# Seven-product FFN units whose products add onto copies that ScalarE writes into PSUM, with PSUM banks in two groups and four changes of order

## The chip, the cores and the metric

The kernel runs on one core of one Trainium2 chip. A core has TensorE (PE: matrix products from SBUF into PSUM; PEld are its weight loads), VectorE (DVE), ScalarE (ACT), GpSimd (POOL) and SyncE (SP), which only issues DMA transfers. Each engine takes its instructions in the order in which they were written for it; engines wait for each other by semaphores. PSUM has 8 banks of 512 fp32 columns in 128 partitions. The metric is the device time of one execution in microseconds. The kernel before takes 1118.08 us, the median of 3 runs (1117.55 to 1118.87).

## The reference

One layer of a decoder trunk over 16 meta tokens and 512 real ones, width 1024, in fp32: an FFN, a token mixer with two attention branches, and a second FFN.

```python
def swiglu(h, w_in, w_out):                      # D_FF = 2816
    gu = h @ w_in                                # (tokens, 1024) @ (1024, 5632)
    gate, up = jnp.split(gu, 2, axis=-1)
    return (jax.nn.silu(gate) * up) @ w_out

def reference(x, meta_tokens, ...):
    ...
    h = h + 0.5 * swiglu(rms_norm(h, ffn1_norm[l]), ffn1_w_in[l], ffn1_w_out[l])
    h = h + token_mixer(rms_norm(h, mix_norm[l]), ...)   # fox and sliding-window attention, gates, w_out
    h = h + 0.5 * swiglu(rms_norm(h, ffn2_norm[l]), ffn2_w_in[l], ffn2_w_out[l])
    return h[:, BLOCK:]                          # the 512 real tokens
```

The gate and up products of both FFNs are the part that the change touches most.

## The kernel before, in words

**Precision.** Every fp32 operand is split into a high part, rounded to the float32r type, and a low part, the rest. `hi` (line 114) is a ScalarE copy with rounding (its instructions show line 117, or 118 with a scale), `lo` (line 120) a VectorE subtraction (line 124, or 126). `prod` (line 246) is three matmuls: high x high (L250), high x low (L251), low x high (L253).

**Weights as pieces.** `pieces` is the list of all weight pieces in the order of use. `load_to` issues their DMA transfers into tiles `raw` (three buffers), `split_to` makes `wh` and `wl` of them (three buffers each), and `piece()` takes the next one, splitting up to three pieces ahead and loading up to five ahead. `tc.issue_after(i)` puts what is written inside it behind instruction `i` on that engine's queue. Apart from that, a planner orders each engine's instructions by the order of the program and by a model of when each can start.

**FFN units.** An FFN makes 22 units of 128 gate and 128 up features for all tokens (528 in the first FFN, 512 in the second). The first 4 (3 in the second FFN) are *plain*: for each half of the tokens, gate and up products over the 1024 input features. The others are *seven-product units* (`Units.unit`, line 448). The tokens are cut into two halves of 264 (256) and the features into two halves of 512, so the input is A11, A12, A21, A22 (token half, feature half), and the weights of the unit are B11, B21 (gate) and B12, B22 (up). Strassen's scheme in Winograd's form makes the 2 x 2 block product in seven products instead of eight, with S1 to S4 for sums of A blocks, which are made once (`Halves.sums`, line 368), and with sums of B blocks, made per unit. Each product is 4 feature blocks x 3 matmuls = 12 matmuls of 264 (256) columns.

The unit's products run in the order A11, A12, S3, S1, S2, A22, S4. P1 = A11 B11 goes to bank b, is copied into SBUF (`p1`, L456) and stays in b, where the S2 product is added to it and gives U2. VectorE then puts the results together: `g` = A12's product + p1, d - p7, minus U2, c + U2, times the SiLU, S4's bank minus U2, times the SiLU: seven operations (`tt`, L450), and the low part of the result. ScalarE does three copies (p1, p7, u2), two SiLUs, and the high part.

**The sums of B blocks.** `sums` (line 177): piece A is the gate block as it is (B11, B21). For B SyncE loads half of the gate and half of the up block side by side into a tile `tb`, and a GpSimd DMA that accumulates adds the 512 KB of the up block onto it (L185). C is made by two VectorE additions (L189, L190), and D is B22.

**PSUM.** One pool of 8 banks serves the whole kernel; `psum()` (line 111) takes the next free one.

**Order around the units.** In `early` (line 647) the plain units are interleaved with the making of the second token half and of S1 to S4, by `weave`, which spreads one list of steps evenly over another. The units come in three groups (8, 8 and 6 units, `KG`), each followed by the product with `w_out` (first FFN lines 705 to 735: 8 output blocks, two banks each; second FFN lines 1410 to 1429: token tiles of 128 x 512 columns, whose results are added to the residual by L1425 and, in the last group, written to `out` in halves of 256 by SyncE and ScalarE queues). In the attention part `fills` (line 1260) lists projection steps that are woven between the steps of the attention: `qb0` and `qb1` are the query projections of the sliding-window branch; the last step of each transposes its normed result. `spread`, `tok_rms`, `features` and `to_features` (lines 304 to 623) make the normed and transposed input at the entry.

Of the kernel before, what the change touches and what calls it, by code (L numbers as in the profile page):

```python
# [73 lines left out]
def kernel(  # L74
# [28 lines left out]
    pp = ctx.enter_context(tc.tile_pool(name="ps", bufs=8, space=PSUM))  # L103
# [7 lines left out]
    def psum():  # L111
        return pp.tile([P, 512], F32, tag="ps", name=nm("ps"))
# [20 lines left out]

    def ffn_pieces(wi, wo, token_major):
        nc_ = NC[token_major]
        for gi, (j0, n) in enumerate(KG):
            for u in range(2 * j0, 2 * (j0 + n)):
                if u < nc_:
                    pieces.extend([("w", [(wi[u], 8, 128)]), ("w", [(wi[NU + u], 8, 128)])])
                else:  # L140
                    pieces.extend([("A", wi[u]), ("B", wi[NU + u]), ("C",), ("D",)])
# [28 lines left out]
    def load(*parts):  # L170
        raw = wp.tile([P, PW], F32, tag="raw", name=nm("raw"))
        for c0, ap in parts:
            i = SP.dma_start(raw[:, c0 : c0 + 128 * ap.shape[1]], ap)
            shared["load"] = getattr(i, "ins", i)
        return raw

    def sums(g, u, gate, up):

        tb_, tc_ = (
            shared["tp"].tile([P, shared["w"]], F32, tag=t, name=nm(t), bufs=2)[:, :1024].rearrange("p (a c) -> p a c", c=512)  # L180
            for t in ("tb", "tc")
        )
        SP.dma_start(tb_[:, 0], gate[:, :4])
        SP.dma_start(tb_[:, 1], up[:, :4])
        G.dma_start(tb_.rearrange("p a c -> p (a c)"), up, accum_op=ALU.add)  # L185

        def rest():
            b21, b22 = g[:, 512:1024], u[:, 512:1024]
            V.tensor_tensor(out=tc_[:, 0], in0=tb_[:, 0], in1=b22, op=ALU.add)  # L189
            V.tensor_tensor(out=tc_[:, 1], in0=tc_[:, 0], in1=b21, op=ALU.add)  # L190
            return tc_.rearrange("p a c -> p (a c)"), 8, 128

        return tb_, rest

    def load_to(n):
        while state["load"] < min(n, len(pieces)):
# [14 lines left out]
            elif kind == "A":  # L211
                shared["g"], shared["gate"] = load((0, what[0])), what[0]
                raws[c] = (shared["g"][:, :1024], 8, 128)
            elif kind == "B":
                g = shared["g"]
                u = load((512, what[0][:, 4:]))
                tb_, rest = sums(g, u, shared["gate"], what[0])
                raws[c] = (tb_.rearrange("p a c -> p (a c)"), 8, 128)
                raws[c + 1] = rest
                raws[c + 2] = (u[:, 512:1024], 4, 128)  # L220

    def split_to(n):
        while state["split"] < min(n, len(pieces)):
# [8 lines left out]
            wh = wp.tile([P, PW], F32R, tag="wh", name=nm("wh"))  # L232
            wl = wp.tile([P, PW], F32R, tag="wl", name=nm("wl"))
# [100 lines left out]
    class Halves:  # L334
# [27 lines left out]
        def diff(self, tag, a, b, op=ALU.subtract):  # L362
            t = shared["tp"].tile([P, shared["w"]], F32, tag=tag, name=nm(tag), bufs=2)
# [4 lines left out]
        def sums(self):  # L368
# [3 lines left out]
            def s3():  # L372

                s["done"] = getattr(self.done, "ins", self.done)
                with tc.issue_after(s["done"]):
                    d = self.diff("tb", self.of(0, 0), self.of(1, 0))
# [7 lines left out]
            def s2():  # L384
                s[2] = self.diff("tb", s[1], self.of(0, 0))
# [7 lines left out]
    class Units:  # L393


        def __init__(self, pool, X):
            self.pool, self.X, self.th = pool, X, X.th
# [17 lines left out]
        def plain(self, dst, mixed):  # L415
# [5 lines left out]
            def part(t, gu, half):  # L421
# [4 lines left out]
                if half == 0:  # L426
                    box["ps", gu] = psum()
# [20 lines left out]
        def unit(self, aH, aL):  # L448
            th = self.th
            tt = lambda o, a, b, op: V.tensor_tensor(out=o, in0=a, in1=b, op=op)  # L450
            u2 = self.new("u2", 1)
            w = piece()
            b, a = psum(), psum()
            self.product(b, "A11", w, 0)
            p1 = self.new("p1", 2)
            A.copy(p1, b[:, :th])  # L456
            self.product(a, "A12", w, 1)
            g = self.new("g", 2)
            tt(g, a[:, :th], p1, ALU.add)
            s1 = self.new("s1", 2)  # L460
# [1034 lines left out]
```

## Time and profile before

| | |
|---|---|
| median of 3 runs | 1118.08 us (1117.55 to 1118.87) |
| the profiled execution | 1117.38 us |
| its span, first to last instruction | 1115.6 us |
| instructions in the span | 20330, of them 8143 matmuls |
| granted TensorE clock | full in all 40 slices |
| GpSimd-issued (accumulating) DMA, queue q0 | 19.48 MB |

The profile is of one execution. A matmul's row shows from when it starts to when its last column is out, so neighbouring rows overlap, and the distance of two starts is the cadence. A row of a group reads: line, engine, operation, output<-inputs by tile name, shape, count | time in all, mean ns of one | idle time of the engine ahead of them, and what ended it. A row of a timeline reads: start us, length us, engine, line, operation, names, shape, count, and in brackets the idle time ahead and what ended it. A row of waits reads: who <- for whom: us in all, times, the longest.

### The profile page before, as it was taken

To read this page: it belongs to the slowest core of one execution; us is meant where nothing else is said; L and a number is where in the kernel's file an instruction comes from. 1 tells how busy PE (TensorE), PEld (TensorE's weight loads), DVE (VectorE), ACT (ScalarE), POOL (GpSimd) and SP (SyncE) were. 2 spreads that over 40 slices of the span, in tenths; PEclk is the share of its full clock that TensorE was granted. 3 is DMA by queue.
4 is the path that set the end of the run, shared out by engine and by line. 5 is a ranking of instruction groups with operands and counts; after the bars stand their busy time and mean duration, and the time that the engine had idled before them with its cause. 6 is when DMAs were issued, how large, how long until landed. Compare 5 with 4: busy or idle time off the path is not lost.

```text
span 1115.6 us, 20330 instructions
## 1 busy us (share of the span) xinstructions
PE 1106.4 (99%) x8143; PEld 1041.2 (93%) x8143; DVE 757.0 (68%) x1416; ACT 527.6 (47%) x941; POOL 84.0 (8%) x119
## 2 busy tenths in 40 slices
PE   8999999999999999999999999999999999999998
PEld 7999999999999999999887888899999899988996
DVE  6757348863687567788877655678685378835872
ACT  6446125541455455456555633355464155623550
POOL 2000000000000321221200000000000000000000
PEclk9999999999999999999999999999999999999999
DMA  7548337872464522212211224455566257733742
GB/s 232 149 128 229 100 95 189 206 221 66 123 162 133 164 77 95 80 58 69 87 57 58 76 76 151 151 177 147 132 173 177 66 159 176 202 125 87 190 131 76
DMA packets 57279, 146.45 MB, mean 131 GB/s; under 512 B 8224, under 2 KB 13344, under 8 KB 57184
## 3 DMA queue, kind: packets, MB, share of 16 engines
q1 hardware_dynamic: 43376, 114.95, 32.1%
q0 software_dynamic: 5456, 19.48, 10.4%
q10 hardware_dynamic: 8352, 10.72, 3.0%
q8 instruction: 64, 1.05, 0.4%
q14 instruction: 31, 0.25, 0.1%
HBM read 140.89 MB, written 6.32 MB: 132 GB/s over the span
## 4 chain that ended last, share of the span: by engine, by line
PE 94%; ACT 2%; DVE 2%; issue 0%; POOL 0%; DVEq 0%; ACTq 0%; POOLq 0%
PE ps L250 29%; PE ps L251 29%; PE ps L253 29%; PE ps L1173 1%; PE ps L1051 1%; PE ps L1006 1%; ACT t L966 1%; PE ps L1066 1%; ACT wh L117 1%; PE ps L288 1%; PE ps L1184 1%; PE ps L1065 0%; PE ps L1185 0%; PE ps L924 0%; DVE wl L124 0%
## 5 line engine op out<-in xcount | busy, mean ns | idle before, releaser
L250 PE MATMUL ps<-x,wh 128*128 128x264 f32 (+2 forms) x1388 | 408.7, 295 | 0.4 <-ACT wh L117 0.3
L251 PE MATMUL ps<-x,wh 128*128 128x264 f32 (+2 forms) x1388 | 407.3, 294 | 0.5 <-DVE x L126 0.4
L253 PE MATMUL ps<-x,wl 128*128 128x264 f32 (+2 forms) x1388 | 406.4, 293 | 0.0
L117 ACT CAST wh<-raw 128x1024 fp32r<-128x1024 f32 (+2 forms) x193 | 183.5, 952 | 246.4 <-PE ps L251 108.4
L124 DVE TENSOR_TENSOR wl<-raw,wh 128x1024 fp32r<-128x1024 f32 (+2 forms) x193 | 212.9, 1104 | 91.2 <-ACT wh L117 89.9
L250 PEld LDWEIGHTS ps<-x,wh 128*128 128x128 f32 x1388 | 261.7, 189 | 7.9 <-ACT x L117 0.8
L251 PEld LDWEIGHTS ps<-x,wh 128*128 128x128 f32 x1388 | 261.3, 188 | 6.0 <-DVE x L126 0.9
L253 PEld LDWEIGHTS ps<-x,wl 128*128 128x128 f32 x1388 | 261.5, 188 | 5.5
L251 PE MATMUL ps<-aL,wh 128*128 128x264 f32 x352 | 93.3, 285 | 0.0
L250 PE MATMUL ps<-aH,wh 128*128 128x264 f32 x352 | 93.1, 285 | 0.0
L250 PE MATMUL ps<-wh,x 128*128 128x256 f32 (+1 forms) x288 | 83.6, 290 | 0.0
L251 PE MATMUL ps<-wl,x 128*128 128x256 f32 (+1 forms) x288 | 81.7, 284 | 0.0
L253 PE MATMUL ps<-wh,x 128*128 128x256 f32 (+1 forms) x288 | 81.3, 282 | 0.0
L253 PE MATMUL ps<-aH,wl 128*128 128x264 f32 x352 | 71.5, 284 | 0.0
L250 PE MATMUL ps<-wh,aH 128*128 128x512 f32 x176 | 69.7, 396 | 0.0
L251 PE MATMUL ps<-wl,aH 128*128 128x512 f32 x176 | 69.2, 393 | 0.0
L253 PE MATMUL ps<-wh,aL 128*128 128x512 f32 x176 | 69.0, 392 | 0.0
L124 DVE TENSOR_TENSOR wl<-tb,wh 128x1024 fp32r<-128x1024 f32 x37 | 45.4, 1226 | 32.9 <-ACT wh L117 31.9
L117 ACT CAST wh<-tb 128x1024 fp32r<-128x1024 f32 x37 | 38.9, 1050 | 59.0 <-PE ps L251 45.7
L251 PEld LDWEIGHTS ps<-aL,wh 128*128 128x128 f32 x352 | 66.2, 188 | 0.1
L250 PEld LDWEIGHTS ps<-aH,wh 128*128 128x128 f32 x352 | 66.2, 188 | 0.0
L721 DVE SCALAR_TENSOR_TENSOR hT<-ps,hT 128x264 f32<-128x264 f32 x48 | 18.6, 427 | 62.1 <-PE ps L253 62.1
(243 smaller groups left out, 1864.6 us busy)
## 6 DMA issues: line engine op xcount, KB each, us to landing
raw<-in_w1i_dram SPq DMA_DIRECT2D x26, 512.0 KB, 3.8
raw<-in_w2i_dram SPq DMA_DIRECT2D x25, 512.0 KB, 3.4
raw<-in_w2o_dram SPq DMA_DIRECT2D x22, 512.0 KB, 4.1
tb<-in_w2i_dram SPq DMA_DIRECT2D x38, 256.0 KB, 3.2
tb<-in_w2i_dram POOLq DMA_DIRECT2D x19, 512.0 KB, 6.9
tb<-in_w1i_dram SPq DMA_DIRECT2D x36, 256.0 KB, 3.5
tb<-in_w1i_dram POOLq DMA_DIRECT2D x18, 512.0 KB, 6.9
raw<-in_wm_dram SPq DMA_DIRECT2D x18, 512.0 KB, 4.2
```

The lines of the kernel that those rows point to most:

```text
L117: return A.copy(o, i)
L124: return V.tensor_tensor(out=o, in0=i, in1=h, op=ALU.subtract)
L250: PE.matmul(ps, sH, mH, start=first, stop=False, **more)
L251: PE.matmul(ps, sH, mL, start=False, stop=False, **more)
L253: shared["mm"] = PE.matmul(ps, sL, mH, start=False, stop=last, **more)
L288: PE.matmul(idle[:, :P], ident, ident, start=True, stop=True)
L721: V.scalar_tensor_tensor(out=hv, in0=p[:, :w], scalar=0.5, in1=hv, op0=ALU.mult, op1=ALU.add)
L966: A.activation(t, t, AF.Exp, bias=nmx, scale=-1.0, accum_out=l[:, j : j + 1])
L1006: PE.matmul(ps[:, :w], q[qx][hb, hp, P * i : P * i + P], k[kx][hb, hp, c0 : c0 + w], start=qx + kx == 0, stop=qx == 1 and not last,)
L1051: PE.transpose(ps[:, c : c + P], ts_[hh][(c // P) % 2][:, c0 : c0 + P], ident)
L1066: PE.matmul(pv[:, a:256], st, pL[:, c0 + a : c0 + 256], start=False, stop=j == nt - 1)
L1173: PE.transpose(ps[:n, P * hh : P * hh + P], ts_[hh][:, c0 : c0 + n], ident)
```

## The change

**The unit** becomes `seven` (products) and a `use` function (what is done with each result). The order of the products is A11, S3, [S4 of the unit before], S2, A22, A12, S1, and S4 is kept pending and done inside the next unit (`flush`). In the last unit of each group the order is S1, A12, S4 at the end. ScalarE copies P1 from bank b into bank a, and the A12 product is added onto the copy. ScalarE writes -U2 into bank d, and the S1 product and later the S4 product are added onto that. VectorE is left with four operations (c + U2, d - p7, two products with a SiLU) and the low part. ScalarE reads one SiLU right from PSUM.

**Banks.** `new_banks(True)` makes two groups of four banks, tags `ps` and `pt`; a and d, onto which ScalarE writes, are from `pt`. The attention part has one pool of eight (`new_banks(False)`), the second FFN two groups again.

**Pieces.** A is now (B11, B12-B22 sum), B the sums made by VectorE, C the loaded block with one sum, D as before. SyncE issues four transfers and GpSimd two accumulating ones of 256 KB a unit. D has its own split buffers (`whD`, `wlD`), the VectorE sums one buffer (`tc`).

**Four changes of order.** The last unit of a group (order of products, and the splits of the next two pieces written behind it); the fills of the attention; one empty step ahead of the S sums of the second FFN; the last token tile of the kernel as two halves of 256 columns in two banks.

```diff
-    pp = ctx.enter_context(tc.tile_pool(name="ps", bufs=8, space=PSUM))
+    def new_banks(split):
+        stP.close()
+        banks["pool"] = stP.enter_context(tc.tile_pool(name=nm("banks"), bufs=4 if split else 8, space=PSUM))
+        banks["split"] = split
+    def psum(whole=False):
+        tag = "pt" if whole and banks["split"] else "ps"
+        return banks["pool"].tile([P, 512], F32, tag=tag, name=nm(tag))
...
+    def load_first(b1, b2, n):
+        raw = wp.tile([P, PW], F32, tag="raw", name=nm("raw"))
+        land(raw, b1[:, :n])
+        land(raw[:, 128 * n :], b2[:, :n])
+        add(raw[:, 128 * n :], b2[:, n:])
+        return raw[:, : 256 * n], 2 * n, 128
+    def load_others(b1, b2, n):
+        w = 128 * n
+        fpool = shared["tp"]
+        c = fpool.tile([P, PW], F32, tag="rawC", name=nm("rawC"), bufs=2)
+        d = fpool.tile([P, 512], F32, tag="rawD", name=nm("rawD"), bufs=2)
+        land(c, b1)
+        add(c, b2[:, :n])
+        land(d, b2[:, n:])
+        def sums():
+            t = fpool.tile([P, PW], F32, tag="tc", name=nm("tc"), bufs=1)
+            V.tensor_tensor(out=t[:, :w], in0=c[:, :w], in1=d[:, :w], op=ALU.add)
+            V.tensor_tensor(out=t[:, w : 2 * w], in0=t[:, :w], in1=c[:, w : 2 * w], op=ALU.add)
+            return t[:, : 2 * w], 2 * n, 128
+        return sums, (c[:, : 2 * w], 2 * n, 128), (d[:, :w], n, 128)
...
+            if pieces[c][0] == "D":
+                wh, wl = (shared["tp"].tile([P, 512], F32R, tag=t, name=nm(t), bufs=1) for t in ("whD", "wlD"))
...
-    def piece():
+    def piece(ahead=None):
...
-        split_to(c + state["ahead"])
+        split_to(c + (ahead or state["ahead"]))
...
-        def unit(self, aH, aL):
...
+        def seven(self, use, last=False):
+            th = self.th
+            w = piece()
+            b, a = psum(), psum(True)
+            self.product(b, "A11", w, 0)
+            A.copy(a[:, :th], b[:, :th])
+            c = psum()
+            self.product(c, "S3", w, 1)
+            use("P7", c[:, :th])
+            self.flush()
+            w = piece()
+            self.product(b, "S2", w, 0, True)
+            d = psum(True)
+            A.activation(d[:, :th], b[:, :th], AF.Identity, scale=-1.0)
+            use("U2", b[:, :th])
+            self.product(c, "A22", w, 1, True)
+            use("C21 - U2", c[:, :th])
+            w = piece()
+            def p2():
+                self.product(a, "A12", w, 1, True)
+                use("C11", a[:, :th])
+            def p5():
+                self.product(d, "S1", w, 0, True)
+                use("C22 + P7", d[:, :th])
+            run([p5, p2] if last else [p2, p5])
+            wd = piece(1 if last else None)
+            def p3():
+                self.product(d, "S4", wd, 0, True)
+                use("C12", d[:, :th])
+            self.pending = p3
+            if last:
+                self.flush()
+        def unit(self, dst, last=False):
+            th, box = self.th, {}
+            tt = lambda o, a, b, op: V.tensor_tensor(out=o, in0=a, in1=b, op=op)
+            def use(what, ps):
+                if what == "P7":
+                    box["p7"] = self.new("p7", 1)
+                    A.copy(box["p7"], ps)
+                elif what == "U2":
+                    box["u2"] = ps
+                elif what == "C21 - U2":
+                    u2 = self.new("u2", 1)
+                    A.copy(u2, box["u2"])
+                    g = self.new("g", 1)
+                    tt(g, ps, u2, ALU.add)
+                    box["s2"] = self.new("s2", 2)
+                    A.activation(box["s2"], g, AF.Silu)
+                elif what == "C11":
+                    box["s1"] = self.new("s1", 2)
+                    A.activation(box["s1"], ps, AF.Silu)
+                elif what == "C22 + P7":
+                    o = box["o"] = self.new("u", 2, 2)
+                    tt(o[:, th:], ps, box["p7"], ALU.subtract)
+                    tt(o[:, th:], o[:, th:], box["s2"], ALU.mult)
+                else:
+                    o = box["o"]
+                    tt(o[:, :th], ps, box["s1"], ALU.mult)
+                    aH, aL = dst
+                    hi(aH, o)
+                    lo(aL, o, aH)
+            self.seven(use, last)
+            if last:
+                split_to(state["use"] + 2)
...
-        pss = [psum() for _ in ks]
+        pss = [psum(k % 2 == 0 or hf == 0 and k == 7) for k in ks]
...
+    new_banks(False)
     kp = ctx.enter_context(tc.tile_pool(name="keep", bufs=1))
...
-        kv[LAG:-1] + qb0[:LAG] + kv[-1:] + qb0[LAG:-1] + qb1[:LAG] + qb0[-1:],
-        qb1[LAG:-1] + gates[:LAG] + qb1[-1:] + gates[LAG : 2 * KD],
+        kv[LAG:-1] + qb0[:LAG] + kv[-1:] + qb0[LAG:-1] + qb1[:2] + qb0[-1:] + qb1[2:4],
+        qb1[4:-1] + gates[:LAG] + qb1[-1:] + gates[LAG : 2 * KD],
...
+    new_banks(True)
     def token_major(i):
...
-    early(X2, ff2, [lambda u=u: act2(u) for u in range(NC[1])], second, X2.sums(), [])
+    early(X2, ff2, [lambda u=u: act2(u) for u in range(NC[1])], second, [nothing] + X2.sums(), [])
...
-            ff2.unit(*act2(u))
+            ff2.unit(act2(u), u == 2 * (j0 + n) - 1)
...
+            ends = [gi == len(KG) - 1 and mq == 1 and i == NB - 1 for i in range(NB)]
+            pss = [[psum(f == 1)[:, :256] for f in range(2)] if e else [psum(i % 2 == 1)] for i, e in enumerate(ends)]
```

More of the change, by code (lines that the diff above doesn't have):

```diff
@@ L132, with seven_pieces @@
     pieces = []
+    def seven_pieces(b1, b2, n):
+        pieces.extend([("A", b1, b2, n), ("B", b1, b2, n), ("C",), ("D",)])
     def ffn_pieces(wi, wo, token_major):
@@ L140, in ffn_pieces @@
                 else:
[L141 removed]
+                    seven_pieces(wi[u], wi[NU + u], 4)
             if token_major:
@@ L168, with land, add @@
     shared = {}
-    def load(*parts):
-        raw = wp.tile([P, PW], F32, tag="raw", name=nm("raw"))
[L172 to L193, printed above, removed]
+    def land(tile_, ap):
+        i = SP.dma_start(tile_[:, : 128 * ap.shape[1]], ap)
+        shared["load"] = getattr(i, "ins", i)
+    def add(tile_, ap):
+        G.dma_start(tile_[:, : 128 * ap.shape[1]], ap, accum_op=ALU.add)
+    def load_first(b1, b2, n):
+        raw = wp.tile([P, PW], F32, tag="raw", name=nm("raw"))
+        land(raw, b1[:, :n])
[16 more added lines that the diff above has]
+        return sums, (c[:, : 2 * w], 2 * n, 128), (d[:, :w], n, 128)
     def load_to(n):
@@ L211, in load_to @@
             elif kind == "A":
-                shared["g"], shared["gate"] = load((0, what[0])), what[0]
-                raws[c] = (shared["g"][:, :1024], 8, 128)
+                raws[c] = load_first(*what)
             elif kind == "B":
[L215 to L220, printed above, removed]
+                raws[c], raws[c + 1], raws[c + 2] = load_others(*what)
     def split_to(n):
@@ L446, in plain, with flush @@
             ]
-        def unit(self, aH, aL):
+        def flush(self):
+            f, self.pending = self.pending, nothing
+            f()
+        def seven(self, use, last=False):
             th = self.th
-            tt = lambda o, a, b, op: V.tensor_tensor(out=o, in0=a, in1=b, op=op)
-            u2 = self.new("u2", 1)
             w = piece()
-            b, a = psum(), psum()
+            b, a = psum(), psum(True)
             self.product(b, "A11", w, 0)
[L455 to L460, printed above, removed]
-            A.activation(s1, g, AF.Silu)
-            w = piece()
-            c, d = psum(), psum()
-            self.product(c, "S3", w, 1)
-            p7 = self.new("p7", 1)
-            A.copy(p7, c[:, :th])
-            self.product(d, "S1", w, 0)
-            o = self.new("u", 2, 2)
-            tt(o[:, th:], d[:, :th], p7, ALU.subtract)
+            A.copy(a[:, :th], b[:, :th])
+            c = psum()
+            self.product(c, "S3", w, 1)
+            use("P7", c[:, :th])
+            self.flush()
@@ L489 @@
+    shared["tp"] = fp
     xn = hT
@@ L695 @@
             later = [residual(u - 3)] if u < 8 else []
-            ff1.unit(*act1(u))
+            ff1.unit(act1(u), u == 2 * (j0 + n) - 1)
             run(later)
@@ L706 @@
             wH, wL = piece()
-            pss = [psum() for _ in hs]
+            pss = [psum(f == 1) for f in range(2)]
             for k in range(nk):
@@ L1424 @@
                     hv = h2[:, i, 512 * mq + c : 512 * mq + c + w]
-                    V.scalar_tensor_tensor(
-                        out=hv, in0=pss[i][:, c : c + w], scalar=0.5, in1=hv, op0=ALU.mult, op1=ALU.add
-                    )
+                    ps = pss[i][1] if ends[i] and c else pss[i][0][:, c : c + w]
+                    V.scalar_tensor_tensor(out=hv, in0=ps, scalar=0.5, in1=hv, op0=ALU.mult, op1=ALU.add)
                     if gi == len(KG) - 1:
```

53 lines of the change are left out of this document (23 added, 30 removed).

## The prediction, made before the changed kernel was run

> **What bounds the kernel now.** I read the first page of the profile first (spans, busy shares, the chain that ended last), then busy time by stretch, then what TensorE waited for, and last the groups of instructions inside a stretch of the seven-product units.
>
> ```profile
> span 1115.6 us, 20330 instructions
> PE 1106.4 (99%) x8143; PEld 1041.2 (93%) x8143; DVE 757.0 (68%) x1416; ACT 527.6 (47%) x941; POOL 84.0 (8%) x119
> ```
>
> ```profile
> PE 94%; ACT 2%; DVE 2%; issue 0%; POOL 0%; DVEq 0%; ACTq 0%; POOLq 0%
> ```
>
> TensorE is busy 1106.4 of 1115.6 us and the chain that ended last lies on it for 94%. So 9.2 us in all are not TensorE time. The stretches tell where they lie, and how full the other engines are in one unit.
>
> ```profile
> 26.50:376.00 349.50, 349.50 (x2872) 349.27 (x2872) 231.86 (x359) 158.93 (x249) 18.77 (x28) 1.00 0.55 151
> 376.00:560.00 184.00, 182.63 (x1531) 173.93 (x1530) 140.00 (x404) 100.10 (x240) 41.59 (x57) 1.00 0.27 83
> 560.00:777.00 217.00, 216.53 (x1271) 186.49 (x1270) 148.34 (x278) 102.51 (x182) 2.34 (x3) 1.00 0.35 112
> 777.00:1111.50 334.50, 334.50 (x2323) 311.14 (x2321) 218.39 (x334) 147.51 (x232) 15.44 (x18) 1.00 0.52 141
> 1111.50:1115.60 4.10, 0.25 (x2) 0.00 (x0) 0.76 (x2) 0.00 (x0) 0.00 (x0) 1.00 0.38 128
> 295.40:305.60 10.20, 10.20 (x86) 10.20 (x85) 8.71 (x15) 6.28 (x12) 0.86 (x1) 1.00 0.47 135
> ```
>
> The last row is from a second answer of the same view. Columns are length, then busy time of TensorE, its weight loads, VectorE, ScalarE and GpSimd, the granted clock, the DMA share. All 37 seven-product units lie in 26.5 to 376 and in 777 to 1111.5 (both FFNs behind their first steps), and there TensorE is busy 349.50 of 349.50 and 334.50 of 334.50 us at a clock of 1.00. The last row is one such unit: TensorE full, VectorE 8.71 of 10.20 us, ScalarE 6.28. VectorE is the fuller of the two, but TensorE never waits for it here. Idle time is left in the attention stretch (1.37 us), in 560 to 777 (0.47), after the last matmul (3.85), and in the first 26.5 us (the remaining 3.5).
>
> ```profile
> PE ps L288 <- POOL ident masks.py:199: 2.2, 1, 2.2
> PE ps L552 <- DVE xt L544: 0.6, 1, 0.6
> PE ps L1065 <- ACT pH L117: 0.6, 1, 0.6
> ```
>
> ```profile
> PE ps L250 <- ACT wh L117: 0.3, 1, 0.3
> PE ps L1006 <- DVE pL L124: 0.3, 1, 0.3
> PE ps L250 <- ACT qH L118: 0.2, 1, 0.2
> ```
>
> These are the waits of TensorE, with their total and number. None belongs to a seven-product unit: the first two are the entry (identity, first token tile), L1065, L1006 and qH the attention, and wh the start of the second FFN.
>
> **The change part by part.** Durations come from one profiled execution, which took 1117.38 us for its span of 1115.6; the median of the three runs shown is 1118.08, 0.70 more. I sum against 1117.38 and add 0.70 at the end.
>
> *The units.* The seven products stay, 12 matmuls each. Matmuls of 264 and of 256 columns follow each other at 0.12 us:
>
> ```profile
> 300.07 0.28 PE L251 MATMUL ps<-x,wh 128*128 128x264 f32 x1
> 300.19 0.28 PE L253 MATMUL ps<-x,wl 128*128 128x264 f32 x1
> ```
>
> ```profile
> 900.09 0.28 PE L251 MATMUL ps<-x,wh 128*128 128x256 f32 x1
> 900.21 0.28 PE L253 MATMUL ps<-x,wl 128*128 128x256 f32 x1
> ```
>
> So a product is 12 x 0.12 = 1.44 us and a unit about 10.1. What goes and comes on the other engines is priced by these rows of the stretch 282 to 346:
>
> ```profile
> L124 DVE TENSOR_TENSOR wl<-tc,wh 128x1024 fp32r<-128x1024 f32 x6 | 7.4, 1226 | 0.8 <-ACT wh L117 0.4
> L450 DVE TENSOR_TENSOR g<-ps,p 128x264 f32<-128x264 f32 x6 | 2.6, 431 | 1.1 <-PE ps L253 0.9
> ```
>
> ```profile
> L117 ACT CAST wh<-tc 128x1024 fp32r<-128x1024 f32 x6 | 6.3, 1049 | 4.9 <-PE ps L251 4.8
> L117 ACT CAST wh<-raw 128x512 fp32r<-128x512 f32 x6 | 3.7, 609 | 1.0 <-PE ps L251 1.0
> L456 ACT COPY p<-ps 128x264 f32<-128x264 f32 x6 | 2.3, 380 | 8.7 <-PE ps L253 8.7
> ```
>
> VectorE loses three operations of 0.43 us, 1.3 a unit and 37 x 1.3 = 48 us in all. ScalarE loses the P1 copy into SBUF and gains two copies into PSUM, so one of 0.38 us more, 14 us in all. Neither reaches TensorE: its 10.20 of 10.20 us has no wait that a freer VectorE could end, and ScalarE has 3.9 us a unit left. The 48 us are worth nothing. A copy from PSUM into PSUM stands in no row; 0.38 (PSUM to SBUF) is the nearest, and the longest ScalarE row, 1.05, is the upper bound I keep; below, even a copy of no time moves nothing.
>
> New are the waits of TensorE for ScalarE. P2 lands on the copy of P1; between A11's product and A12's lie S3, the late S4 of the unit before, S2 and A22, four products or 5.8 us, for a copy of 0.38. S1 lands on -U2: between lie A22 and A12, 2.9 us. In the last unit of a group S1 comes right behind A22, and 1.44 us are left. ScalarE is in order: behind a late copy stand the P7 or U2 copy, a weight cast and the SiLU, and VectorE waits for those. Ahead of -U2 stands at most the cast of the 512-wide piece, 0.61 us, whose data are old by then. 0.61 + 0.38 = 1.0 us is below 1.44, so I take 0. The bound above: a 1.05 cast is slipped in between as well, 2.04 - 1.44 = 0.6 us, and if the copy takes 1.05 too, 1.3. Six groups: 3.6 to 7.6 us; no gain is possible, as TensorE is full.
>
> *The weights.* SyncE still issues four transfers a unit, with the same bytes. Instead of one accumulating transfer of 512 KB GpSimd issues two of 256 KB.
>
> ```profile
> q0 software_dynamic: 5456, 19.48, 10.4%
> ```
>
> ```profile
> tb<-in_w2i_dram POOLq DMA_DIRECT2D x19, 512.0 KB, 6.9
> ```
>
> One lands after 6.9 us. Two halves cost between 2 x 3.45 (time goes by bytes) and 2 x 6.9 = 13.8 us, if they go one behind the other. Their queue fills 10.4% of the DMA engines' time, 116 us or 3.1 us a unit, so most of 6.9 is latency, which overlaps. With two buffers for C and D and three for the first piece, the queue runs more than a unit ahead; I take 0. The Trainium skill (DMA: Bandwidth & Descriptors, Anatomy of one DMA) gives a GpSimd transfer a fixed 2.0 us beside its bytes, which speaks against cutting one in two: an estimate by it is 3.2 us for 512 KB and 2 x 2.6 = 5.2 for the halves, 2.0 more a unit. Its 3.2 differs from the 6.9 measured here, and on the end it would put 0 as well, as 5.2 is below a unit's 10.
>
> The other edits of the pieces (an own buffer for the split of D, one for the sums) shorten waits of casts and touch no row of TensorE: 0.
>
> *Banks.* Two groups of four hold what eight held: a unit takes two of each. Where the pools are replaced, the first bank taken may be the one read last:
>
> ```profile
> 381.97 0.29 PE L794 MATMUL ps<-wh,xm 128*128 128x264 f32 x1
> ...
> 382.05 0.77 DVE L721 SCALAR_TENSOR_TENSOR hT<-ps,hT 128x264 f32<-128x264 f32 x2 [0.85 <-PE ps L253]
> ```
>
> ```profile
> 760.20 0.28 PE L250 MATMUL ps<-x,wh 128*128 128x256 f32 x1
> ...
> 760.40 0.42 DVE L1341 TENSOR_TENSOR h2T<-h2T,ps 128x256 f32<-128x256 f32 x1 [0.18 <-PE ps L253]
> ```
>
> The projection starts at 381.97 and the second FFN at 760.20, before the last bank of the stage ahead is read. If the bank is the wrong one, TensorE waits until 382.82 (0.85 us) and 760.82 (0.6). Bounds 0 and 1.45; few of the banks are affected, and I take 0.3 + 0.1 = +0.4.
>
> *Later sums in the second FFN.* The 0.3 us wait for wh stands behind a cast of the S3 operand:
>
> ```profile
> 774.48 1.06 ACT L117 CAST x<-tb 128x1024 fp32r<-128x1024 f32 x1 [2.43 <-DVE tb L365]
> 775.44 1.99 ACT L117 CAST wh<-raw 128x1024 fp32r<-128x1024 f32 x2
> ```
>
> ```profile
> 776.53 0.39 PE L250 MATMUL ps<-x,wh 128*128 128x256 f32 x1 [0.31 <-ACT wh L117]
> ```
>
> With S3 some steps later the weight cast comes 1 us sooner: -0.3. S3 and S2 are needed sooner in the new order, but not before the first seven-product unit, which follows the three plain ones. Bounds -0.3 and +0.5 (half of a cast the other way).
>
> *Attention order.* One step of qb1 goes behind the finish of qb0, and one more moves into the second stage. Three waits lie there, 0.6, 0.3 and 0.2. I take -0.4, the qH wait and part of the others; bounds -1.1 (all) and +1.1, as the finish now comes one step sooner behind the norms it needs.
>
> *The end.* The last token tile's 18 matmuls of 512 columns become 36 of 256, and its first half is read while the second is computed.
>
> ```profile
> 1111.12 0.40 PE L251 MATMUL ps<-wl,aH 128*128 128x512 f32 x1
> 1111.36 0.40 PE L253 MATMUL ps<-wh,aL 128*128 128x512 f32 x1
> ```
>
> ```profile
> 1111.79 0.76 DVE L1425 SCALAR_TENSOR_TENSOR h<-ps,h 128x256 f32<-128x256 f32 x2 [0.65 <-PE ps L253]
> ```
>
> 512 columns take 0.24 us, twice the 0.12 of 256, so the 36 cost what the 18 did. Behind the last matmul there is one operation where two took 0.76; by the single one of 0.42 at 760.40 that is -0.34, rounded to -0.3.
>
> **Sum:** 0 + 0 + 0.4 - 0.3 - 0.4 - 0.3 = -0.6. 1117.38 - 0.6 = 1116.8 for such an execution, 1117.5 against the median. A measurement of this kernel can tell 0.2% from no change, 2.2 us; this is a quarter of that.
>
> **The rivals.** *Gain:* the reordering takes away all of the idle time between 376 and 777 (1.84 us), the end gives 0.3 and the entry, whose banks are dealt anew, its 0.6 for the token tile: -2.7, so 1115.3. For it: the reordered steps are the ones at the waits. Against it: several of these waits (0.6 for pH) are not at the steps that are moved.
>
> *Slower:* the copy of -U2 in the last unit of each group. It decides from the point where the copy ends later than 1.44 us behind S2's last matmul. With a 1.05 cast ahead of it and a copy of 0.61 (as the 512-wide cast, if PSUM as a target is dearer) the wait is 0.61 + 1.05 + 0.61 - 1.44 = 0.83 us, six times 5.0, so 1122.5. For it: ScalarE does place casts in the gaps between copies. Against it: ScalarE is idle 3.9 us in each unit.
>
> *Accumulates in a row:* if two halves take 13.8 us one behind the other, every unit lasts 13.8 instead of 10.1, 37 x 3.7 = 137 us more, 1255. The 10.4% speak against it. By the fixed 2.0 us of the Trainium skill's page above it doesn't come about either.
>
> *Not as it says:* the planner may put the late S4 elsewhere; as every order fills TensorE, that is the forecast again.
>
> **How the numbers follow.** Forecast 0.70, gain 0.15, slower 0.13, accumulates 0.02. The forecast's own bounds against the median: at best 1118.08 + 0 - 0.3 - 1.1 - 0.3 = 1116.4, at worst 1118.08 + 1.45 + 0.5 + 1.1 - 0.3 = 1120.8. 0.2% either way is 1115.8 to 1120.3, so nearly all of the forecast is no change; I move 0.02 of it to each side for what I have not priced. Faster 0.15 + 0.02 = 0.17, same 0.66, slower 0.13 + 0.02 + 0.02 = 0.17. The range goes from the gain's 1115.3 to the forecast's worst, 1120.8; about 0.07 is left out below and 0.13 above.
>
> **What would show it.** Right: TensorE busy about 1106.5 with the same full stretches, VectorE about 48 us lighter and ScalarE about 14 heavier, no wait of TensorE for a ScalarE copy, only one VectorE operation behind the last matmul. Wrong: rows of TensorE released by the new copies or by VectorE's reading in the last units, waits at the first matmuls behind the replaced pools, or a sum of waits between 376 and 560 that is above 1.4 us.

## The result and the profile after

The changed kernel takes 1123.88 us, the median of 6 runs (1123.64 to 1125.42), against 1118.92 (1117.55 to 1119.36) of the kernel before on the same chip. The ratio is 1.0049, its 95% interval 1.0036 to 1.0062: slower by half a per cent. The forecast was no change, 1117.5, and the range ended at 1120.8. The profiled execution took 1123.78 us; its span, from the first to the last instruction, is 1122.0, 6.4 more than before.

The first page of the changed kernel, busy time and the chain that ended last:

```profile
span 1122.0 us, 20389 instructions
PE 1107.4 (99%) x8161; PEld 1042.1 (93%) x8161; DVE 716.1 (64%) x1305; ACT 534.5 (48%) x978; POOL 115.9 (10%) x156
...
PE 92%; ACT 2%; DVE 2%; DMA 2%; issue 1%; POOL 0%; SPq 0%; ACTq 0%; DVEq 0%; POOLq 0%
```

VectorE is lighter by 40.9 us, ScalarE heavier by 6.9, and TensorE is busy for the same time within 1 us. What is new is in the chain: 2% lie on DMA, which is not in the line of before. Busy time of both FFN stretches (length, then TensorE, weight loads, VectorE, ScalarE, GpSimd):

```profile
26.50:376.00 349.50, 347.08 (x2844) 346.04 (x2843) 209.03 (x301) 159.17 (x263) 33.45 (x45) 1.00 0.55 148
...
777.00:1111.50 334.50, 333.69 (x2340) 311.22 (x2339) 198.55 (x273) 153.21 (x252) 31.81 (x37) 1.00 0.52 139
```

Both were full before; now TensorE is idle 2.42 and 0.81 us in them. The waits of TensorE in the whole span:

```profile
PE pt L270 <- DVE u L518: 1.6, 2, 1.1
PE ps L270 <- ACT pt L482: 1.6, 2, 1.3
...
PE ps L859 <- ACT wh L128: 0.8, 1, 0.8
PE ps L270 <- DVE h2T L1406: 0.6, 1, 0.6
```

The first two lie in the second seven-product unit of each FFN, the other two are the first matmuls behind the replaced pools. (For the first of these the row names a weight cast; e3 and e10 below show that the projection does not need that cast.) Where the time went shows best when the start of the same matmul, by its number, is set beside that of before (us; e7 and e10 are experiments below):

| matmul | place | before | after | e7 | e10 |
|---|---|---|---|---|---|
| 500 | first FFN, first seven-product units | 68.60 | 68.65 | 68.28 | 69.11 |
| 600 | the second one behind | 80.69 | 83.66 | 80.50 | 81.36 |
| 3000 | end of the first FFN | 372.96 | 376.29 | 372.92 | 373.63 |
| 3100 | projection begun | 385.15 | 389.58 | 386.21 | 385.84 |
| 4600 | behind the reordered attention | 567.72 | 571.34 | 568.57 | 567.72 |
| 5600 | before the second FFN | 749.39 | 753.00 | 750.24 | 749.41 |
| 5700 | second FFN begun | 761.25 | 765.71 | 762.94 | 761.28 |
| 5900 | its plain units | 786.21 | 789.66 | 786.90 | 786.23 |
| 6100 | its second seven-product unit | 809.88 | 814.86 | 810.77 | 810.09 |
| 8000 | late in its last units | 1078.42 | 1083.93 | 1079.82 | 1079.49 |
| last | start of the last one | 1111.36 | 1117.01 | 1112.90 | 1112.57 |

Differences of the two columns, and of these from row to row, make the bill: **+2.9** at the second seven-product unit of the first FFN, +0.4 up to its end, **+1.1** at the projection's start, -0.8 in the attention, **+0.85** at the start of the second FFN, -1.0 behind it, **+1.5** at its second seven-product unit, +0.7 in small steps up to the last matmul, and +0.8 behind that. Together 6.4. (e10's profiled run is the slowest of its 11, and it is 0.5 us late at matmul 500 already; from row to row its column can be read like the others.)

**The second unit.** In the stretch at 62 to 82 us VectorE's queue reads (start, length, line, names, and in brackets the idle time ahead):

```profile
62.59 1.23 DVE L135 TENSOR_TENSOR wl<-tc,wh 128x1024 fp32r<-128x1024 f32 x1 [3.38 <-ACT wh L128]
63.85 1.26 DVE L385 TENSOR_TENSOR tc<-hT,rawC 128x1056 f32<-128x1056 f32 x1
...
76.55 0.69 DVE L213 TENSOR_TENSOR tc<-rawC,rawD 128x512 f32<-128x512 f32 x1 [5.49 <-DMA rawC<-in_w1i_dram]
77.27 0.69 DVE L214 TENSOR_TENSOR tc<-tc,rawC 128x512 f32<-128x512 f32 x1
77.88 0.42 DVE L518 TENSOR_TENSOR u<-pt,p 128x264 f32<-128x264 f32 x1
```

SyncE, then GpSimd, in the same stretch:

```profile
65.14 1.95 SPq L187 DMA_DIRECT2D rawC<-in_w1i_dram  x2
```

```profile
69.01 0.86 POOL L191 DMA_DIRECT2D rawC<-in_w1i_dram  x1 [9.17 <-DVE aL L135]
```

And ScalarE:

```profile
78.05 1.05 ACT L128 CAST wh<-tc 128x1024 fp32r<-128x1024 f32 x1 [5.65 <-DVE tc L214]
...
79.95 1.06 ACT L733 COPY hT<-ps 128x512 f32<-128x512 f32 x2
80.91 0.39 ACT L482 COPY pt<-ps 128x264 f32<-128x264 f32 x1
```

Read it backwards. The copy of P1 (L482) stands behind a weight cast that waited 5.65 us for the sums of B blocks, behind one more cast and behind two copies of the residual. The S2 product is added onto P1 in the bank that this copy reads, so it has to wait for the copy and starts 1.27 us late. The same sums stand ahead of d - p7 (L518, 77.88) in VectorE's queue, which delays the S4 product by 1.12. The sums waited 5.49 us for the accumulating transfer, which was issued at 69.01 onto a load that SyncE could issue only at 65.14. Till then both `rawC` buffers were held: one by the first unit, one by the S2 sum, which is released when the S4 sum (L385, 63.85) has read it. That one needs the single `tc`, which the first unit's sums held until their low part was made (62.59 to 63.82). One buffer of sums and two of loads are shared by the S operands and the first two units. Once the S operands are made, this does not come back: no later unit is among the waits.

### The profile page after: what moved, and what is told of

It is laid out like the page before. It is cut to its first block, busy times and chain, and to the rows that moved or that the text cites. A ratio compares the mean times of both kernels' runs of the same rounds, so it can differ in the third digit from the quotient of the medians.

```text
span 1122.0 us, 20389 instructions
## 1 busy us (share of the span) xinstructions
PE 1107.4 (99%) x8161; PEld 1042.1 (93%) x8161; DVE 716.1 (64%) x1305; ACT 534.5 (48%) x978; POOL 115.9 (10%) x156
## 3 DMA queue, kind: packets, MB, share of 16 engines
q8 instruction: 64, 1.05, 0.4%
## 4 chain that ended last, share of the span: by engine, by line
PE 92%; ACT 2%; DVE 2%; DMA 2%; issue 1%; POOL 0%; SPq 0%; ACTq 0%; DVEq 0%; POOLq 0%
PE ps L270 19%; PE ps L271 19%; PE ps L273 19%; PE pt L270 9%; PE pt L271 9%; PE pt L273 9%; ACT wh L128 1%; PE ps L1116 1%; PE ps L1238 1%; PE ps L1071 1%; DMA rawC<-in_w2i_dram 1%; PE ps L1131 1%; DMA rawC<-in_w1i_dram 1%; ACT t L1031 1%; DVE wl L135 1%
## 5 line engine op out<-in xcount | busy, mean ns | idle before, releaser
L128 ACT CAST wh<-raw 128x1024 fp32r<-128x1024 f32 (+3 forms) x156 | 160.9, 1032 | 270.7 <-PE pt L271 79.4
L135 DVE TENSOR_TENSOR wl<-raw,wh 128x1024 fp32r<-128x1024 f32 (+3 forms) x156 | 187.7, 1203 | 142.1 <-ACT wh L128 141.5
L270 PE MATMUL ps<-x,wh 128*128 128x264 f32 (+2 forms) x832 | 252.5, 304 | 2.3 <-ACT pt L482 1.6
L271 PE MATMUL ps<-x,wh 128*128 128x264 f32 (+2 forms) x832 | 249.9, 300 | 0.5 <-DVE x L137 0.4
L273 PE MATMUL ps<-x,wl 128*128 128x264 f32 (+2 forms) x832 | 249.5, 300 | 0.0
L270 PEld LDWEIGHTS ps<-x,wh 128*128 128x128 f32 x832 | 157.0, 189 | 9.6 <-ACT pt L482 2.0
L271 PEld LDWEIGHTS ps<-x,wh 128*128 128x128 f32 x832 | 156.9, 189 | 5.8 <-DVE x L137 0.9
L273 PEld LDWEIGHTS ps<-x,wl 128*128 128x128 f32 x832 | 156.8, 188 | 5.5
L273 PE MATMUL pt<-x,wl 128*128 128x264 f32 (+1 forms) x408 | 115.5, 283 | 0.0
L271 PE MATMUL pt<-x,wh 128*128 128x264 f32 (+1 forms) x408 | 115.5, 283 | 0.0
L270 PE MATMUL pt<-x,wh 128*128 128x264 f32 (+1 forms) x408 | 115.4, 283 | 0.0
L270 PEld LDWEIGHTS pt<-x,wh 128*128 128x128 f32 x408 | 77.0, 189 | 1.0 <-ACT x L128 1.0
L271 PEld LDWEIGHTS pt<-x,wh 128*128 128x128 f32 x408 | 76.9, 189 | 0.0
L273 PEld LDWEIGHTS pt<-x,wl 128*128 128x128 f32 x408 | 76.9, 188 | 0.0
```

The costliest lines, as they stand in the source:

```text
L128: return A.copy(o, i)
L135: return V.tensor_tensor(out=o, in0=i, in1=h, op=ALU.subtract)
L270: PE.matmul(ps, sH, mH, start=first, stop=False, **more)
L271: PE.matmul(ps, sH, mL, start=False, stop=False, **more)
L273: shared["mm"] = PE.matmul(ps, sL, mH, start=False, stop=last, **more)
```

## The experiments

The short names are those of the runs. Each ratio is to the kernel before on the same chip. e5 to e8 ran on another chip than e1 to e4, e9 and e10, so between these two sets it is the ratios that compare.

**e1: the S4 sum in place.**

```diff
-                self.parts("S4", self.diff("tc", self.of(0, 1), s[2], ALU.add))
+                V.tensor_tensor(out=s[2], in0=self.of(0, 1), in1=s[2], op=ALU.add)
+                self.parts("S4", s[2])
```

> Changed kernel, with one edit: the sum for S4 is written onto the tile of the S2 sum and no longer takes the single tc buffer. Theory (a chain of buffers): the loaded block of the second seven-product unit comes late because its rawC buffer is held until the S4 sum has read the S2 sum, and the S4 sum waits for tc, which the VectorE sums of the first unit hold. Then the transfer starts some 8 us sooner, the waits of TensorE in the second unit (1.1 and 1.3 us in the first FFN, 0.5 and 0.3 in the second) go, and the time falls by 3.5 to 4.5 us to about 1119.7. Rival (the accumulating transfers are slow as such): the waits stay within 0.5 us. Rival (the order on VectorE and ScalarE is the cause, whenever the data come): they stay, as the order there is kept.

Measured: 1121.04 us, ratio 1.0025 (1.0016 to 1.0035), 2.8 us less than the changed kernel. The loss at the second unit of the first FFN is gone (matmul 600 at 80.76, before 80.69). That of the second FFN is still there:

```profile
PE pt L270 <- DVE u L519: 1.4, 1, 1.4
```

So the chain over `tc` is the cause in the first FFN, and in the second something else is enough to make the wait. Its SyncE, GpSimd and VectorE queues there:

```profile
791.26 1.49 SPq L187 DMA_DIRECT2D raw<-in_w2i_dram  x1
792.85 7.08 SPq L187 DMA_DIRECT2D rawC<-in_w2i_dram  x2
```

```profile
798.39 0.85 POOL L191 DMA_DIRECT2D raw<-in_w2i_dram  x1 [5.43 <-ACT wh L128]
799.62 0.85 POOL L191 DMA_DIRECT2D rawC<-in_w2i_dram  x1 [0.38 <-DVE wl L135]
```

```profile
806.10 0.69 DVE L213 TENSOR_TENSOR tc<-rawC,rawD 128x512 f32<-128x512 f32 x1 [3.63 <-DMA rawC<-in_w2i_dram]
```

First pieces (`raw`) of later units stand ahead of the `rawC` transfers that the second unit needs sooner, on SyncE's queue and on GpSimd's; from the accumulate at 799.62 it is 6.5 us until the sums can start.

**e2: the sums behind d - p7 on VectorE.**

```diff
-                with tc.issue_after(shared["lo"]):
-                    raw = raw()
+                with ExitStack() as st:
+                    st.enter_context(tc.issue_after(shared["lo"]))
+                    if "dp7" in shared:
+                        st.enter_context(tc.issue_after(shared["dp7"]))
+                    raw = raw()
...
-                    tt(o[:, th:], ps, box["p7"], ALU.subtract)
+                    i = tt(o[:, th:], ps, box["p7"], ALU.subtract)
+                    shared["dp7"] = getattr(i, "ins", i)
```

> Changed kernel, with one edit: on VectorE the two additions for the next unit stand behind the unit's own d - p7 in place of ahead of it; the transfers are as late as before. If the order on VectorE makes the wait of S4's product (1.1 us in the first FFN, 0.5 in the second): that wait goes. The wait for ScalarE's copy into PSUM (1.3 and 0.3), which stands behind the cast of the late sums, stays or grows. Time 1.0 to 1.7 us less. If the late transfer alone counts, the time that is saved at S4 is lost again at that copy, and the sum of both stays at 2.4 and 0.8.

Measured: 1126.1 us, 1.0075 (1.0052 to 1.0098), slower than the changed kernel in the median of 4 runs, whose scatter (1123.93 to 1130.02) is wide; the profile is of the slowest. No wait for `u` is left, but

```profile
PE ps L273 <- ACT wh L128: 2.2, 1, 2.2
PE ps L736 <- DMA xr<-in_x_dram: 1.5, 2, 0.8
PE ps L273 <- ACT pt L485: 1.2, 1, 1.2
```

The 1.2 is in the second seven-product unit of the first FFN, the 2.2 in that of the second; between matmul 500 and 600 this run loses 2.3 us, the changed kernel 2.9, and between 5900 and 6100 3.7 against 1.5. What is late is the data. To let d - p7 pass hands most of the wait on to the copy and the weight cast, and the later units lose some 0.1 us each besides (1.6 us from matmul 680 to 2820, where the changed kernel loses 0.4). The order in VectorE's queue is where the lateness shows, not where it comes from.

**e3: no pool replaced.** Two groups of four for the whole kernel; the attention takes from them in turn.

```diff
-        tag = "pt" if whole and banks["split"] else "ps"
+        if banks["split"]:
+            tag = "pt" if whole else "ps"
+        else:
+            banks["n"] = banks.get("n", 0) + 1
+            tag = "pt" if banks["n"] % 2 else "ps"
...
-    new_banks(False)
+    banks["split"] = False
```

> Changed kernel, with one edit: the pools are not replaced around the attention; the attention takes its banks from the two groups in turn. Theory (the first bank of a new pool is the one that was read last): the waits of TensorE at the first matmul of the projection (0.84 us) and of the second FFN (0.60) go, 1.4 us less, 1122.4. Rival (the projection waits for a weight cast, as the profile's row names it): 0.84 stays. The attention, whose banks come in another order, may move by 0.5 either way.

Measured: 1122.09 us, 1.0039 (1.0024 to 1.0053). Both waits at the first matmuls are gone; the projection starts with no idle time, while the weight cast that the row of the changed kernel names has only begun (384.74 to 385.79). So the rival falls:

```profile
384.78 0.29 PE L863 MATMUL pt<-wh,xm 128*128 128x264 f32 x1
```

But the attention, whose banks are dealt otherwise, lost 2.5 us against the changed kernel between matmul 3100 and 4600 (387.95 to 572.18, there 389.58 to 571.34). So the gain of the dealing could not be read from the total; e10 does that.

**e4: no split of the last tile.**

```diff
-            ends = [gi == len(KG) - 1 and mq == 1 and i == NB - 1 for i in range(NB)]
+            ends = [False for i in range(NB)]
```

> Changed kernel, with one edit: the last token tile is computed in one bank of 512 columns again. In the changed kernel the last transfer was issued 0.45 us sooner behind the last matmul than before, but took 3.1 us to land in place of 1.9. If the split as such makes those transfers slow (they come closer together), they land within 2 us here and the time behind the last matmul's start falls from 5.0 to 4.2 us, 0.8 less in all. If the 3.1 us are chance, this kernel is up to 0.45 us slower or the same.

Measured: 1123.64 us, 1.0043 (1.0027 to 1.0058): no difference to the changed kernel that can be told. Behind the end of the last matmul before has 3.80 us and e4 4.10; the split tile has 3.44 in the profiles of e7, e8, e9 and e10, and 4.71 in that of the changed kernel, where the last two transfers to `out` landed 3.26 and 3.13 us after their issue instead of 1.8 to 2.3. This happened in three of the ten profiled kernels with the split (changed, e1, e5), so the split as such is not the cause. What makes them late isn't settled; it is 1.3 us of the profiled execution.

**e5: the transfers in order of use.** On SyncE's and GpSimd's queues a unit's first piece stands behind the other pieces of the unit before.

```diff
-        G.dma_start(tile_[:, : 128 * ap.shape[1]], ap, accum_op=ALU.add)
+        i = G.dma_start(tile_[:, : 128 * ap.shape[1]], ap, accum_op=ALU.add)
+        shared["add"] = getattr(i, "ins", i)
...
-        land(raw, b1[:, :n])
-        land(raw[:, 128 * n :], b2[:, :n])
-        add(raw[:, 128 * n :], b2[:, n:])
+        with ExitStack() as st:
+            if "others" in shared:
+                for k in ("others", "others_add"):
+                    st.enter_context(tc.issue_after(shared[k]))
+            land(raw, b1[:, :n])
+            land(raw[:, 128 * n :], b2[:, :n])
+            add(raw[:, 128 * n :], b2[:, n:])
...
         land(c, b1)
+        shared["others"] = shared["load"]
         add(c, b2[:, :n])
+        shared["others_add"] = shared["add"]
```

> The changed kernel with one thing more: on SyncE's and GpSimd's queues the transfers of a unit's first piece stand behind those of the other pieces of the unit before. The sums of the S operands and their buffers stay as in the changed kernel. Theory 'buffer first, then queue': in both FFNs the buffer of the second unit's other pieces comes free only behind the S4 sum (63.9 and 799.6 us in the changed kernel), so order alone helps little: the wait in the first FFN stays near 2.9 us and that in the second at 1 to 1.5, 1122.5 to 1124. Rival 'queue alone': the transfers are late only because first pieces stand ahead of them; then both waits shrink below 0.5 us and the time is about 1119.5.

Measured: 1124.07 us, 1.0056 (1.0042 to 1.0069), as "buffer first, then queue" has it. Both waits stay:

```profile
PE pt L277 <- DVE u L525: 2.8, 2, 1.5
...
PE ps L277 <- ACT pt L489: 1.6, 2, 1.3
```

**e6: the banks dealt on.**

```diff
     new_banks(False)
+    for _ in range(4):
+        V.memset(psum()[:, :1], 0.0)
...
     new_banks(True)
+    for _ in range(1):
+        V.memset(psum()[:, :1], 0.0)
```

> The changed kernel with its two replaced pools, but behind each replacement dummy tiles (four, and one) are written by VectorE with one column, so that the first real tile no longer lies in the bank that was read last (bank 0 both times); every engine's order is the same but for these small VectorE operations. Theory 'the bank': both waits (1.10 us of drift at 385 us, 0.85 at 761 us) vanish, nothing in the attention moves, 1123.9 - 1.9 = 1122.0. Rival 'any replaced pool waits for the whole one before': both waits stay and the time is 1124. If the loss of the run with one pool in the attention came from dealing and not from chance, the attention here keeps its -0.6 us.

Measured: 1122.43 us, 1.0050 (1.0034 to 1.0066), but single runs from 1120.27 to 1125.65, so the total can't choose between 1122.0 and 1124. By the allocation the first tile now lies in bank 1 (projection) and bank 3 (second FFN); in the changed kernel it lay in bank 0 both times, which had been read last ahead of the second FFN, and last but one ahead of the projection. Yet matmul 3100 and 5700 lose 1.10 and 0.85 us, to the hundredth what they lost. VectorE's last reads and TensorE's first matmul at the projection:

```profile
383.75 0.43 DVE L785 SCALAR_TENSOR_TENSOR hT<-ps,hT 128x264 f32<-128x264 f32 x1 [0.86 <-PE ps L273]
384.10 0.42 DVE L785 SCALAR_TENSOR_TENSOR hT<-pt,hT 128x264 f32<-128x264 f32 x1
```

```profile
384.67 0.36 PE L861 MATMUL ps<-wh,xm 128*128 128x264 f32 x1 [0.84 <-ACT wh L128]
```

It starts 0.15 behind the end of the last read of the old pool, which is not of its bank. The changed kernel starts 0.15 behind that read, too (386.34, the read ends at 386.19), so the four small VectorE operations in between add nothing. My theory of the bank falls; "any replaced pool waits for the whole one before" stands.

**e7: sum in place, transfers in order, banks dealt on** (the edits of e1, e5 and e6).

> The changed kernel with three repairs: the S4 sum is written onto the S2 sum, the transfers stand in the order of use as in e5, and the banks are dealt on as in e6. Theory 'buffer, queue and banks make the loss': no wait of TensorE is left at the second seven-product unit of either FFN (2.9 and 1.5 us in the changed kernel) nor at the two first matmuls (1.1 and 0.85), 1123.9 - 2.9 - 1.5 - 1.9 = 1117.6, the same as before within 0.2%. Rival for the second FFN, 'the S sums themselves come too late there': the wait at its second unit stays above 1 us although the transfers are in order, and the time is about 1119.5.

Measured: 1118.23 us, 0.9999 (0.9990 to 1.0008): before again, with the new units. In the second FFN the accumulates now stand in the order of use and the sums start at 802.37, 3.7 us sooner than in e1. GpSimd and VectorE:

```profile
797.86 0.85 POOL L191 DMA_DIRECT2D rawC<-in_w2i_dram  x1 [12.26 <-DVE u L465]
799.13 0.85 POOL L191 DMA_DIRECT2D raw<-in_w2i_dram  x1 [0.42 <-issue]
```

```profile
802.37 0.68 DVE L220 TENSOR_TENSOR tc<-rawC,rawD 128x512 f32<-128x512 f32 x1
```

No seven-product unit is among the waits any more; at the second unit of the second FFN 0.2 us are left of the 1.5 to 1.9. e1 shows what the buffer alone gives, e5 what the order alone gives (nothing), e7 that the second FFN needs both. (e10 below has both without the dealing of banks, and 0.2 us are left there as well.)

**e8: e7 with three more VectorE multiplications a unit.** Their results go to scratch and are read by nothing.

```diff
+                    for _ in range(3):
+                        x_ = self.new("g", 1)
+                        tt(x_, o[:, th:], box["s2"], ALU.mult)
```

> e7 with three more VectorE multiplications of 0.43 us a unit into a scratch tile that nothing reads, 37 units: as many operations on VectorE as the kernel before had. Theory 'VectorE's seven operations are not what bounds a unit': 48 us more of VectorE time, the time within 1 us of e7. Rival 'the freed operations are worth something that the waits hid': e7 is faster than before by 1 us or more and this run loses it again, 1.5 us or more slower than e7.

Measured: 1117.94 us, 1.0000 (0.9991 to 1.0009). VectorE is as full as before the change, and TensorE does not notice. Busy time of the first FFN (VectorE is the third):

```profile
26.50:376.00 349.50, 349.50 (x2871) 349.08 (x2870) 232.99 (x359) 161.52 (x264) 34.24 (x46) 1.00 0.55 149
```

**e9: before with three of the order changes** (the fills, the empty step, the split of the last tile).

```diff
-    early(X2, ff2, [lambda u=u: act2(u) for u in range(NC[1])], second, X2.sums(), [])
+    early(X2, ff2, [lambda u=u: act2(u) for u in range(NC[1])], second, [nothing] + X2.sums(), [])
...
```

> The kernel before with three of the four order changes and nothing else of the change: the fills of the attention, the empty step ahead of the S sums of the second FFN, the last token tile as two halves in two banks. Its units, pieces and single pool are those of before. Theory 'the order changes gain by themselves and the rest of the change only costs': attention -0.6 (the changed kernel's drift from 421 to 761 us), start of the second FFN -0.5 to -1.0, end -0.5, so 1118.1 - 1.6 to 2.1, about 1116.3. By the prediction's terms (-0.4, -0.3, -0.3) 1117.1. Rival 'the second FFN's gain belongs to the new order of the units': 0 there, 1117.0 to 1117.5.

Measured: 1117.21 us, 0.9993 (0.9984 to 1.0002). The attention gives 0.5 (from +0.28 at matmul 3100 to -0.24 at 4600), the end 0.4, the empty step nothing: the wait that it should shorten is still 0.3.

```profile
PE ps L250 <- ACT wh L117: 0.3, 1, 0.3
```

**e10: e7 with one pool of eight** in place of groups and replaced pools.

```diff
-        banks["pool"] = stP.enter_context(tc.tile_pool(name=nm("banks"), bufs=4 if split else 8, space=PSUM))
+        banks["pool"] = stP.enter_context(tc.tile_pool(name=nm("banks"), bufs=8, space=PSUM))
...
-        tag = "pt" if whole and banks["split"] else "ps"
+        tag = "ps"
...
-    new_banks(False)
...
-    new_banks(True)
```

> e7 without the two groups of banks: one pool of eight for the whole kernel, as before the change, so no pool is replaced; the S4 sum in place and the transfers in order of use stay. Theory 'a replaced pool makes its first matmul wait for the last read of all its banks, whichever bank is dealt': the drifts of 1.1 us at 386 us and 0.85 us at 763 us vanish and the attention keeps its gain, 1118.2 - 1.95 = 1116.3. Rival 'the units need their two groups': without them the copies into PSUM wait for a bank, TensorE loses some tenths of a us in each of 37 units, 1118 or more.

Measured: 1117.28 us, 0.9991 (0.9982 to 1.0000). The units don't need two groups. The projection follows without a wait, while VectorE still reads the banks of the stage ahead:

```profile
382.68 0.29 PE L866 MATMUL ps<-wh,xm 128*128 128x264 f32 x1
```

```profile
382.75 0.77 DVE L793 SCALAR_TENSOR_TENSOR hT<-ps,hT 128x264 f32<-128x264 f32 x2 [0.86 <-PE ps L280]
```

By the ratios the gain over e7 is 0.9 us, not the 1.95 I expected, and the two intervals overlap, so its size is not sure. The rows say more. At the projection (matmul 3000 to 3100) e7 loses 1.1 us against before and e10 nothing. At the start of the second FFN e7 loses 0.85 (5600 to 5700) and has 1.0 back by 5900; e10 loses and regains nothing. There TensorE waits a little later anyway (in e10 0.17 us for `sqacc`, 0.31 for a weight cast), and e7, which starts late, has neither wait. So that pool's wait is hidden, and only the projection's 1.1 counts. Neither e9 nor e10 is faster by the 0.2% that can be told from no change.

## Why the prediction was wrong, and where it was right

**The weights failed.** "With two buffers for C and D and three for the first piece, the queue runs more than a unit ahead; I take 0" holds in the steady units and not in the second one of each FFN, where the S operands hold those buffers. And "the other edits of the pieces (an own buffer for the split of D, one for the sums) shorten waits of casts and touch no row of TensorE: 0" overlooked that the one buffer `tc` (the kernel before had two) is also the S4 sum's. Both terms were 0; together they cost 2.9 and 1.5 us, 4.4 of the 6.4 (shown by e1 for the first FFN, by e1, e5 and e7 for the second). I looked at bytes and queue share, and did not write down who holds each buffer when the first units begin.

**Banks: the mechanism was another, the size the upper bound.** With "few of the banks are affected" the sum took 0.4 of 1.45. Both first matmuls waited in full (0.84 and 0.60 idle, +1.1 and +0.85 in starts), whichever bank was dealt (e6), and not at all where no pool is replaced (e3, e10). In the total only the first counts.

**Later sums: -0.3 was nothing.** e9 keeps the wait. The 1.0 us that the changed kernel regains there belongs to the pool's late start.

**Attention and end were right in size, as far as can be told.** -0.4 against -0.5 in e9 and -0.8 in the changed kernel; but e7 and e8, with the same attention, show -0.2 and -0.8, so a single profile does not settle this term. -0.3 against -0.4 where the last transfers land as usual. The list of waits that the attention's term was taken from left out one of 0.2 us there.

**The units were right in the main.** The 48 us were worth nothing, as said: VectorE lost 40.9, and e8 gives it 43.7 back (759.6 against 715.9 of e7) without a change in time. (It is not 48, nor ScalarE's 6.9 the 14, in part because neighbouring rows overlap: 77.27 + 0.69 above is past 77.88.) No last unit of a group waits for -U2, so the slower rival was at the wrong place; the kernel was slower, but by another chain. "No wait of TensorE for a ScalarE copy" was wrong in the row (1.6 us for L482), though the copy itself takes 0.40 at most: it stands behind a late cast. I had looked at the products that land on a copy, and not at those that land in a bank which a copy must read first. No kernel here sends P1 through SBUF in the new order, so what the copies alone give is not separated; with all repairs the new units are worth nothing that can be measured.

**Small steps at the ends of the groups.** The +0.7 of the second FFN is still there in e10, which loses 1.05 us from matmul 5900 to 8000; 0.85 of it lies in six places. In the first unit of a group no S4 of the unit before stands between S3 and S2. So A22, which is added onto S3's bank, comes before ScalarE has copied P7 out of that bank, as a weight cast stands ahead of this copy (e10, second group, ScalarE and TensorE):

```profile
897.68 1.05 ACT L128 CAST wh<-raw 128x1024 fp32r<-128x1024 f32 x1 [0.99 <-PE ps L278]
898.63 0.36 ACT L531 COPY p<-ps 128x256 f32<-128x256 f32 x1
```

```profile
898.86 0.28 PE L280 MATMUL ps<-x,wl 128*128 128x256 f32 x1
899.05 0.39 PE L277 MATMUL ps<-x,wh 128*128 128x256 f32 x1
```

A22 starts 0.05 us behind the end of the copy, and so it does in the first units of all six groups of e10; it costs 0.17 to 0.19 us in each of the three of the second FFN. In the last units of the three groups S4 starts 0.06 to 0.10 behind VectorE's d - p7, which costs 0.08 to 0.12 us each. So the ends of the groups do cost, as the slower rival had it, but at P7 and d - p7 in place of -U2, and some 0.3 us a group in place of its 0.83. In the first FFN of the changed kernel the same places cost 0.17, 0.30 and 0.20 us (at matmuls 1262, 1886 and 2318), and some of that is given back later. This is read from the traces; no run takes it away.

**Still open:** what makes the last transfers late, and whether two `tc` buffers alone would have spared the first FFN its wait; no run tries that.

## What to carry to other kernels

Before a term is set to 0 because a queue runs ahead, list for each shared buffer who holds it at the start of the phase, not in its middle: a start-up that borrows the buffers of the steady loop sets when the first loads go out. When a fuller engine never delays the one that bounds the time, taking work off it buys nothing, and what the edit adds in waits is the whole effect. A wait at an in-order engine has to be followed back to the data, since a new order alone only moves it.

## What was not expected of the hardware

An accumulating transfer of half the size did not take half the time. 512 KB landed in 6.9 us before; the 256 KB of the changed kernel take, in the median (issues by GpSimd, count, size, us to landing):

```profile
rawC<-in_w2i_dram POOLq DMA_DIRECT2D x19, 256.0 KB, 4.8
raw<-in_w2i_dram POOLq DMA_DIRECT2D x19, 256.0 KB, 4.3
...
rawC<-in_w1i_dram POOLq DMA_DIRECT2D x18, 256.0 KB, 5.2
raw<-in_w1i_dram POOLq DMA_DIRECT2D x18, 256.0 KB, 4.5
```

and the late one of the first FFN, in the chain of waits:

```profile
69.01 7.46 DMA rawC<-in_w1i_dram
```

By the Trainium skill (DMA: Bandwidth & Descriptors, Anatomy of one DMA) a half would be an estimated 2.6 us; no row here agrees with that for accumulating transfers.

Some kernels that keep a late transfer scatter: e6 ran from 1120.27 to 1125.65 in 4 runs, and in its profiled run, the fastest, the second units lose 1.6 and 0.8 us in place of 2.9 and 1.5. e7, without late transfers, ran from 1117.32 to 1118.62 in 11. But the changed kernel (1123.64 to 1125.42 in 6) and e5 (1123.68 to 1124.60 in 4) keep both late transfers and scatter little, so the cause of the scatter is not shown.
